# DoRA forward on one core: weights loaded first, weight preparation on 128 partitions, more buffers, equal blocks

## The chip, the core and the metric

The kernel runs on one core of a Trainium2 chip. The core has a matrix engine (TensorE, "PE" in the profile, its weight loads as "PEld"), a vector engine (VectorE, "DVE"), a scalar engine (ScalarE, "ACT"), GpSimd ("POOL") and a synchronising engine ("SP"). Matrix results go to PSUM, everything else lives in SBUF; transfers between SBUF and the chip's main memory are done by 16 DMA engines. In this kernel two engines issue transfers: SP, whose transfers the profile shows as queue q1, and ACT, whose transfers are q10. The metric is the device time of one execution in microseconds (us); smaller is better.

## The reference

```python
# x: 16 x 2048 x 256, W: 256 x 256, lora_A: 256 x 16, lora_B: 16 x 256, m: 256, scale = 1.0, all float32
W_adapted = W + scale * (lora_A @ lora_B)
W_norm = np.sqrt(np.sum(W_adapted ** 2, axis=0, keepdims=True) + 1e-8)
W_final = W_adapted / W_norm * m
y = x.reshape(-1, 256) @ W_final          # 32768 x 256 times 256 x 256
```

The input x and the output y have 33.55 MB each. The weights have 0.28 MB together. So the kernel reads x once, writes y once, and multiplies by a small matrix that it must first prepare.

## The kernel before

**Weight preparation.** Four transfers bring `lora_A` (`a_nat`, as 256 pieces of 64 bytes), `W` (`w_nat`, 256 pieces of 1 KB), `lora_B` (`b_nat`) and `m` (`m_row`, one row on one partition). PE transposes `a_nat` (L92), multiplies with `lora_B` (L98), DVE adds `W` (L107, `wa`), ACT squares (L112), PE sums over the rows with a column of ones (L115, one row of 256 sums on one partition), ACT takes the square root (L119), DVE the reciprocal (L120) and the product with `m` (L121), PE spreads the row over 128 partitions with a row of ones (L123), and DVE multiplies `wa` by it (L127) into `w_final`, 128 x 2 x 256 in bf16.

**Main loop.** x is cut into blocks. A full block is 2048 rows (2 MB): each of 128 partitions takes 16 consecutive rows, so one contiguous piece of 16 KB. A block is loaded by one transfer on SP (L71 for the first, L141 for the others) into one of the `xpool` buffers. It is worked off in groups of 4 rows per partition ("chunks", four to a full block, 64 in all). For each chunk PE makes 8 transposes (L151) into a PSUM tile `xt_ps` (two of them), DVE casts it to bf16 into `xt_sb` (L157, `xtpool` buffers), PE makes 8 matmuls with `w_final` (L162) into `y_ps` (two), and ACT copies it to the block's output tile `y_sb` (L169). After a block's last chunk ACT issues the store of the block (L171) out of one of the `ypool` buffers. Before, there are 4 load buffers, 12 `xt_sb` and 3 store buffers. The list `blocks` cuts the last 2048 rows into three pieces of 8, 4 and 4 rows per partition (pieces of 8 KB and 4 KB, `x_sb_1443`, `x_sb_1489` and `x_sb_1514` in the order below); the 15 blocks ahead of them are full. Blocks are counted from 0 here, chunks from 1.

**What sets the order.** The program is written block by block, and a scheduler turns it into one fixed list of instructions per engine. Each engine works its list strictly in order. The scheduler lets PE's transposes run ahead of the matmuls as far as the buffers reach: 12 `xt_sb` plus 2 `xt_ps` before. A transpose that waits for a load therefore also holds up the matmuls of older chunks that stand behind it. In the same way a copy on ACT that waits for a free `y_sb` buffer holds up everything behind it on ACT, and a load on SP waits until the transposes of the block that had its buffer are done.

Of the kernel before, what the change touches and what calls it, by code (L numbers as in the profile page):

```python
# [10 lines left out]
@with_exitstack  # L11
def kernel(
    ctx: ExitStack,
    tc: tile.TileContext,
    x: bass.AP,
    W: bass.AP,
    lora_A: bass.AP,
    lora_B: bass.AP,
    m: bass.AP,
    scale: float,  # L20
    out: bass.AP,
):
# [22 lines left out]
    off = (NBLK - n_tail) * DJ  # L45
    tail_js = n_tail * DJ
    pieces = [8] * (tail_js // 8 - 1) + [4, 4]
    for dj in pieces:
        blocks.append((off * P, dj))
        off += dj  # L50
# [9 lines left out]
    identity = consts.tile([P, P], FP32)  # L60
    make_identity(nc, identity)
    ones_col = consts.tile([P, 1], FP32)
    nc.vector.memset(ones_col, 1.0)  # L63
    ones_row = consts.tile([1, P], FP32)
    nc.vector.memset(ones_row, 1.0)

    w_final = consts.tile([P, KC, OUT], BF16)

    x_sb_first = xpool.tile([P, DJ, IN], FP32, name="x_sb", tag="x_sb")
    dj0 = blocks[0][1]  # L70
    nc.sync.dma_start(  # L71
        out=x_sb_first[:, :dj0, :],
        in_=x_flat[0 : dj0 * P].rearrange("(p j) k -> p j k", p=P),
    )
# [9 lines left out]
    eps_1 = startup.tile([1, 1], FP32)  # L84
    nc.vector.memset(eps_1, 1e-8)

    b_bf = startup.tile([R, OUT], BF16)
    nc.vector.tensor_copy(out=b_bf, in_=b_nat)

    aT_ps = pp_y.tile([R, KC * P], FP32, tag="psy", name="aT_ps")  # L90
    for c in range(KC):
        nc.tensor.transpose(aT_ps[:, c * P : (c + 1) * P], a_nat[:, c, :], identity)  # L92
    aT = startup.tile([R, KC * P], BF16)
    nc.vector.tensor_copy(out=aT, in_=aT_ps)  # L94

    ab_ps = pp_y.tile([P, KC, OUT], FP32, tag="psy", name="ab_ps")
    for c in range(KC):
        nc.tensor.matmul(  # L98
            ab_ps[:, c, :],
            aT[:, c * P : (c + 1) * P],  # L100
            b_bf,
            start=True,
            stop=True,
        )

    wa = startup.tile([P, KC, OUT], FP32)
    nc.vector.scalar_tensor_tensor(  # L107
        out=wa, in0=ab_ps, scalar=float(scale), in1=w_nat, op0=ALU.mult, op1=ALU.add
    )
# [4 lines left out]
    for c in range(KC):  # L114
        nc.tensor.matmul(  # L115
            n2_ps, ones_col, sq[:, c, :], start=(c == 0), stop=(c == KC - 1)
        )
    d_row = startup.tile([1, OUT], FP32)
    nc.scalar.activation(out=d_row, in_=n2_ps, func=AF.Sqrt, bias=eps_1)  # L119
    nc.vector.reciprocal(out=d_row, in_=d_row)  # L120
    nc.vector.tensor_mul(out=d_row, in0=d_row, in1=m_row)  # L121
    db_ps = pp_y.tile([P, OUT], FP32, tag="psy", name="db_ps")
    nc.tensor.matmul(db_ps, ones_row, d_row, start=True, stop=True)  # L123
    d_bcast = startup.tile([P, OUT], FP32)
    nc.vector.tensor_copy(out=d_bcast, in_=db_ps)  # L125
    for c in range(KC):
        nc.vector.tensor_mul(out=w_final[:, c], in0=wa[:, c], in1=d_bcast)  # L127

    j_order = []
    for a in range(J // 2):  # L130
        j_order.append(a)
        j_order.append(a + J // 2)

    for s0, dj in blocks:
        nsub = dj // J

        if s0 == 0:
            x_sb = x_sb_first
        else:
            x_sb = xpool.tile([P, DJ, IN], FP32, name="x_sb", tag="x_sb")  # L140
            nc.sync.dma_start(  # L141
                out=x_sb[:, :dj, :],
                in_=x_flat[s0 : s0 + dj * P].rearrange("(p j) k -> p j k", p=P),
            )
        y_sb = ypool.tile([P, DJ, OUT], FP32, name="y_sb")

        for c in range(nsub):
            xt_ps = pp_xt.tile([P, KC, J * P], FP32, tag="psxt", name="xt_ps")
            for j in range(J):
                for kc in range(KC):  # L150
                    nc.tensor.transpose(  # L151
                        xt_ps[:, kc, j * P : (j + 1) * P],
                        x_sb[:, c * J + j, kc * P : (kc + 1) * P],
                        identity,
                    )
            xt_sb = xtpool.tile([P, KC, J * P], BF16, name="xt_sb")
            nc.vector.tensor_copy(out=xt_sb, in_=xt_ps)  # L157

            y_ps = pp_y.tile([P, J, OUT], FP32, tag="psy", name="y_ps")
            for kc in range(KC):  # L160
                for j in j_order:
                    nc.tensor.matmul(  # L162
                        y_ps[:, j, :],
                        xt_sb[:, kc, j * P : (j + 1) * P],
                        w_final[:, kc, :],
                        start=(kc == 0 and (j % (J // 2)) == 0),
                        stop=(kc == KC - 1 and (j % (J // 2)) == (J // 2) - 1),
                    )
            nc.scalar.copy(out=y_sb[:, c * J : (c + 1) * J, :], in_=y_ps)  # L169

        nc.scalar.dma_start(  # L171
            out=out_flat[s0 : s0 + dj * P].rearrange("(p j) k -> p j k", p=P),
            in_=y_sb[:, :dj, :],
        )


# [33 lines left out]
```

## Time and profile before

| What | us |
|---|---|
| Median of 3 runs (lowest, highest) | 174.78 (174.4, 175.59) |
| Span of the profiled execution, first to last instruction | 172.6 |
| Median less that span | 2.2 |
| PE busy / DVE busy / ACT busy | 131.4 / 80.1 / 65.5 |
| First matmul with the finished weights | 24.93 |
| First store issued | 30.11 |
| PE's last wait for a load ends | 142.90 |
| Last store issued | about 168.0 |

The profiled execution has no time of its own on record beside its span; what lies around the span is taken as the difference to the median, 2.2 us (1.8 to 3.0 by the lowest and highest run). In the profile's strip of 40 slices a slice is 4.3 us wide and a digit is the busy share in tenths. In rows of a timeline the first number is the start, the second the time to the end of the group, and what stands in brackets is the idle time of the engine ahead of it and what ended it.

### The profile page before, as it was taken

How to read it: one execution, taken by the hardware profiler on the slowest of the kernel's cores; microseconds unless marked ns; L12 is line 12 of the kernel's file. 1: busy time of each engine (PE TensorE's matmuls, PEld its weight loads, DVE VectorE, ACT ScalarE, POOL GpSimd, SP SyncE). 2: the span in 40 equal slices, each digit the busy share in tenths (PEclk: the TensorE clock that was granted, in tenths of full speed). 3: DMA queues.
4: the chain of work that ended last, by engine and by line, in shares of the span. 5: the costliest groups of instructions: out<-in, count | busy, mean ns of one | idle time of the engine just before them, and what ended most of it. 6: DMA issues, size and time to landing. Idle time of an engine off the chain costs nothing.

```text
span 172.6 us, 2407 instructions
## 1 busy us (share of the span) xinstructions
PE 131.4 (76%) x1034; PEld 109.6 (64%) x1034; DVE 80.1 (46%) x75; ACT 65.5 (38%) x68; POOL 0.7 (0%) x6
## 2 busy tenths in 40 slices
PE   0089589899998989989898989889689408898300
PEld 0077468777786878868787878777578407676200
DVE  0046991792948558465555656565355500500000
ACT  2004008417062350807180808163428000898320
POOL 1000000000000000000000000000000000000000
PEclk9999999999999999999999999999999855999955
DMA  5999999999999999999999999999999970299985
GB/s 179 415 417 425 429 433 421 421 429 433 421 418 418 429 425 425 429 435 425 429 429 425 425 444 429 423 425 429 431 426 418 446 299 0 122 421 421 433 345 206
DMA packets 5772, 67.55 MB, mean 391 GB/s; under 512 B 881, under 2 KB 1154, under 8 KB 1666
## 3 DMA queue, kind: packets, MB, share of 16 engines
q1 hardware_dynamic: 2898, 33.84, 46.8%
q10 hardware_dynamic: 2864, 33.57, 45.9%
q8 instruction: 8, 0.13, 0.3%
q14 instruction: 2, 0.02, 0.0%
HBM read 33.85 MB, written 33.55 MB: 391 GB/s over the span
## 4 chain that ended last, share of the span: by engine, by line
PE 50%; DMA 24%; DVE 14%; ACT 7%; issue 2%; ACTq 0%
PE xt_ps L151 25%; PE y_ps L162 24%; DMA x_sb<-in_x_dram 14%; DVE xt_sb L157 13%; ACT y_sb L169 7%; DMA out_dram<-y_sb 5%; DMA a_nat<-in_lora_A_dram 5%; DVE d_row L120 1%; PE n_ps L115 1%; PE db_ps L123 0%; PE aT_ps L92 0%; PE ab_ps L98 0%; ACTq L171 0%; ACTq L169 0%
## 5 line engine op out<-in xcount | busy, mean ns | idle before, releaser
L157 DVE CAST xt_sb<-xt_ps 128x1024 bf16<-128x1024 f32 x64 | 76.0, 1220 | 59.5 <-PE xt_ps L151 33.1
L169 ACT COPY y_sb<-y_ps 128x1024 f32<-128x1024 f32 x64 | 61.9, 1015 | 88.5 <-PE y_ps L162 78.1
L151 PE MATMUL xt_ps<-identity,x_sb 128*128 128x128 f32 x512 | 72.3, 286 | 17.4 <-DVE xt_sb L157 8.5
L151 PEld LDWEIGHTS xt_ps<-identity,x_sb 128*128 128x128 f32 x512 | 59.1, 146 | 28.0 <-DVE xt_sb L157 19.9
L162 PE MATMUL y_ps<-w_final,xt_sb 128*128 128x256 bf16 x512 | 63.7, 276 | 3.3 <-ACT y_sb L169 3.3
L162 PEld LDWEIGHTS <-xt_sb 128*128 128x128 bf16 x512 | 50.6, 99 | 13.3 <-issue 6.4
L92 PE MATMUL aT_ps<-identity,a_nat 128*16 128x128 f32 x2 | 0.6, 394 | 9.1 <-DMA a_nat<-in_lora_A_dram 9.1
L92 PEld LDWEIGHTS aT_ps<-identity,a_nat 128*16 128x16 f32 x2 | 0.1, 90 | 9.1 <-issue 9.1
L112 ACT ACTIVATE sq<-wa 128x512 f32<-128x512 f32 x1 | 0.6, 631 | 10.8 <-DVE wa L107 10.8
L94 DVE CAST aT<-aT_ps 16x256 bf16<-16x256 f32 x1 | 0.4, 412 | 8.7 <-PE aT_ps L92 8.7
L112 ACT ACT_TABLE_LOAD x1 | 1.3, 1283 | 1.2 <-PEq L191 1.2
L120 DVE RECIPROCAL d_row<-d_row 1x256 f32<-1x256 f32 x1 | 1.7, 1730 | 0.0
L119 ACT ACT_TABLE_LOAD x1 | 1.3, 1283 | 0.0
L119 ACT ACTIVATE d_row<-n_ps,eps 1x256 f32<-1x256 f32 x1 | 0.5, 465 | 1.9 <-PE n_ps L115 1.9
L115 PE MATMUL n_ps<-sq,ones_col 128*1 128x256 f32 x4 | 1.0, 378 | 0.0
L127 DVE TENSOR_TENSOR w_final<-wa,d_bcast 128x256 bf16<-128x256 f32 x2 | 0.8, 417 | 0.0
L123 PE MATMUL db_ps<-d_row,ones_row 1*128 1x256 f32 x2 | 0.7, 426 | 0.0
L107 DVE SCALAR_TENSOR_TENSOR wa<-ab_ps,w_nat 128x512 f32<-128x512 f32 x1 | 0.7, 681 | 0.0
L98 PE MATMUL ab_ps<-b_bf,aT 16*128 16x256 bf16 x2 | 0.6, 402 | 0.0
L115 PEld LDWEIGHTS n_ps<-sq,ones_col 128*1 128x1 f32 x4 | 0.3, 82 | 0.4 <-issue 0.2
L63 DVE MEMSET ones_col<- 128x1 f32 x1 | 0.1, 59 | 0.8 <-PEq L191 0.8
L125 DVE COPY d_bcast<-db_ps 128x256 f32<-128x256 f32 x1 | 0.4, 402 | 0.0
(12 smaller groups left out, 2.2 us busy)
## 6 DMA issues: line engine op xcount, KB each, us to landing
x_sb<-in_x_dram SPq DMA_DIRECT2D x15, 2048.0 KB, 16.2
out_dram<-y_sb ACTq DMA_DIRECT2D x15, 2048.0 KB, 15.1
x_sb<-in_x_dram SPq DMA_DIRECT2D x1, 1024.0 KB, 28.2
x_sb<-in_x_dram SPq DMA_DIRECT2D x2, 512.0 KB, 24.9
out_dram<-y_sb ACTq DMA_DIRECT2D x1, 1024.0 KB, 9.2
out_dram<-y_sb ACTq DMA_DIRECT2D x2, 512.0 KB, 3.7
w_nat<-in_W_dram SPq DMA_DIRECT2D x1, 256.0 KB, 8.2
a_nat<-in_lora_A_dram ACTq DMA_DIRECT2D x1, 16.0 KB, 8.3
```

What stands on the lines that cost most here:

```text
L92: nc.tensor.transpose(aT_ps[:, c * P : (c + 1) * P], a_nat[:, c, :], identity)
L107: nc.vector.scalar_tensor_tensor(out=wa, in0=ab_ps, scalar=float(scale), in1=w_nat, op0=ALU.mult, op1=ALU.add)
L112: nc.scalar.activation(out=sq, in_=wa, func=AF.Square)
L115: nc.tensor.matmul(n2_ps, ones_col, sq[:, c, :], start=(c == 0), stop=(c == KC - 1))
L119: nc.scalar.activation(out=d_row, in_=n2_ps, func=AF.Sqrt, bias=eps_1)
L120: nc.vector.reciprocal(out=d_row, in_=d_row)
L123: nc.tensor.matmul(db_ps, ones_row, d_row, start=True, stop=True)
L127: nc.vector.tensor_mul(out=w_final[:, c], in0=wa[:, c], in1=d_bcast)
L151: nc.tensor.transpose(xt_ps[:, kc, j * P : (j + 1) * P], x_sb[:, c * J + j, kc * P : (kc + 1) * P], identity,)
L157: nc.vector.tensor_copy(out=xt_sb, in_=xt_ps)
L162: nc.tensor.matmul(y_ps[:, j, :], xt_sb[:, kc, j * P : (j + 1) * P], w_final[:, kc, :], start=(kc == 0 and (j % (J // 2)) == 0), stop=(kc ...
L169: nc.scalar.copy(out=y_sb[:, c * J : (c + 1) * J, :], in_=y_ps)
```

## The change

Transfers: `w_nat` is issued first on SP, ahead of the first block of x. `b_nat` and `m_row` move from SP to ACT's queue, behind `a_nat`.

Weight preparation: it is scheduled with high priority. `m` is spread over 128 partitions at once by a product of one row of ones with `m_row` (L92, `mb_ps`, copied to `m_all` at L94). The square is done by DVE (L111). The sum over rows is done with a full 128 x 128 matrix of ones (L116), so that every partition holds all 256 sums; the square root (L120) and the reciprocal (L125) then run on 128 partitions, and the second spreading product is gone. `wa` times `m` (L123, `wam`) is computed ahead of the reciprocal, and `w_final` is `wam` times the reciprocal (L127). ACT makes one square root on a dummy (L77) at the start, which loads its function table there.

Buffers: six load buffers for four, five store buffers for three, six `xt_sb` for twelve. Blocks: all 16 are full blocks; the three small pieces at the end are gone. Nothing else of the main loop is changed (transposes L142, casts L148, matmuls L153, copies L160, stores L162, loads L53 in the new numbering).

```diff
-    n_tail = min(1, NBLK)
-    blocks = [(i * BLK, DJ) for i in range(NBLK - n_tail)]
...
-    pieces = [8] * (tail_js // 8 - 1) + [4, 4]
...
-    xpool = ctx.enter_context(tc.tile_pool(name="xpool", bufs=4))
-    xtpool = ctx.enter_context(tc.tile_pool(name="xtpool", bufs=12))
-    ypool = ctx.enter_context(tc.tile_pool(name="ypool", bufs=3))
+    xpool = ctx.enter_context(tc.tile_pool(name="xpool", bufs=6))
+    xtpool = ctx.enter_context(tc.tile_pool(name="xtpool", bufs=6))
+    ypool = ctx.enter_context(tc.tile_pool(name="ypool", bufs=5))
...
-    nc.sync.dma_start(out=b_nat, in_=lora_B)
+    nc.scalar.dma_start(out=b_nat, in_=lora_B)
     m_row = startup.tile([1, OUT], FP32)
-    nc.sync.dma_start(out=m_row, in_=m[None, :])
...
+    nc.scalar.dma_start(out=m_row, in_=m[None, :])
...
+    ones = consts.tile([P, P], FP32)
+    nc.vector.memset(ones, 1.0)
...
+    nc.scalar.activation(out=warm, in_=eps_col, func=AF.Sqrt)
...
+    with tc.high_priority():
...
+        mb_ps = pp_y.tile([P, OUT], FP32, tag="psy", name="mb_ps")
+        nc.tensor.matmul(mb_ps, ones[0:1, :], m_row, start=True, stop=True)
+        m_all = startup.tile([P, OUT], FP32)
+        nc.vector.tensor_copy(out=m_all, in_=mb_ps)
...
-    sq = startup.tile([P, KC, OUT], FP32)
-    nc.scalar.activation(out=sq, in_=wa, func=AF.Square)
-    n2_ps = pp_y.tile([1, OUT], FP32, tag="psy", name="n2_ps")
...
+        sq = startup.tile([P, KC, OUT], FP32)
+        nc.vector.tensor_mul(out=sq, in0=wa, in1=wa)
...
+        n2_ps = pp_y.tile([P, OUT], FP32, tag="psy", name="n2_ps")
+        for c in range(KC):
+            nc.tensor.matmul(
+                n2_ps, ones, sq[:, c, :], start=(c == 0), stop=(c == KC - 1)
+            )
+        norm = startup.tile([P, OUT], FP32)
+        nc.scalar.activation(out=norm, in_=n2_ps, func=AF.Sqrt, bias=eps_col)
+        wam = startup.tile([P, KC, OUT], FP32)
+        for c in range(KC):
+            nc.vector.tensor_mul(out=wam[:, c], in0=wa[:, c], in1=m_all)
+        rnorm = startup.tile([P, OUT], FP32)
+        nc.vector.reciprocal(out=rnorm, in_=norm)
+        for c in range(KC):
+            nc.vector.tensor_mul(out=w_final[:, c], in0=wam[:, c], in1=rnorm)
...
-    for s0, dj in blocks:
...
+    for b in range(NBLK):
+        x_sb = load_x(b)
```

Three places of the fixed lists are used below: SP's list, the start of PE's list and the end of PE's list. First SP's list from its start, which holds only transfers (`128x4096` is a full block, `128x2048` and `128x1024` are the small pieces):

```order
-L71 DMA x_sb<-in_x_dram 128x4096
-L79 DMA w_nat<-in_W_dram 128x2x256
-L81 DMA b_nat<-in_lora_B_dram 16x256
-L83 DMA m_row<-in_m_dram 1x256
-L141 DMA x_sb<-in_x_dram 128x4096 x14
-L141 DMA x_sb<-in_x_dram 128x2048
-L141 DMA x_sb<-in_x_dram 128x1024 x2
-L205 UNCONDITIONAL_BRANCH
+L196 UNCONDITIONAL_BRANCH
+L63 DMA w_nat<-in_W_dram 128x2x256
+L53 DMA x_sb<-in_x_dram 128x4096 x16
```

The first block now stands behind `w_nat`, the two small transfers have left SP, and the last 2048 rows come as one load.

Second, PE's list from its start up to the first matmul with the finished weights, before (`x8` and the like count rows that follow each other):

```order
L92 MATMUL aT_ps<-identity,a_nat 16x128 x2
L151 MATMUL xt_ps<-identity,x_sb 128x128 x8
L98 LDWEIGHTS aT
L98 MATMUL ab_ps<-b_bf,aT 128x256
L98 LDWEIGHTS aT
L98 MATMUL ab_ps<-b_bf,aT 128x256
L151 MATMUL xt_ps<-identity,x_sb 128x128 x23
L115 MATMUL n_ps<-sq,ones_col 1x256 x2
L151 MATMUL xt_ps<-identity,x_sb 128x128 x20
L123 MATMUL db_ps<-d_row,ones_row 128x256
L151 MATMUL xt_ps<-identity,x_sb 128x128 x15
```

and now:

```order
L87 MATMUL aT_ps<-identity,a_nat 16x128 x2
L92 MATMUL mb_ps<-m_row,ones 128x256
L98 LDWEIGHTS aT
L98 MATMUL ab_ps<-b_bf,aT 128x256
L98 LDWEIGHTS aT
L98 MATMUL ab_ps<-b_bf,aT 128x256
L142 MATMUL xt_ps<-identity,x_sb 128x128 x9
L116 MATMUL n_ps<-sq,ones 128x256 x2
L142 MATMUL xt_ps<-identity,x_sb 128x128 x18
```

Before, 66 transposes of x stand ahead of the first matmul with the weights, spread between the steps of the preparation; now 27 do, and all of them stand behind the product that needs `m_row` (L92).

Third, the place on PE where the transposes of the last rows stand, before. `y_ps_1214` is the 50th of 64 chunks, and the last row of it is the first row here; `x_sb_1514` is the last piece loaded; `y_ps_1235` is chunk 51.

```order
L162 MATMUL y_ps_1214<-w_final_85,xt_sb_1212 128x256
L151 MATMUL xt_ps_1446<-identity_76,x_sb_1443 128x128 x7
L151 MATMUL xt_ps_1467<-identity_76,x_sb_1443 128x128 x8
L151 MATMUL xt_ps_1492<-identity_76,x_sb_1489 128x128 x8
L151 MATMUL xt_ps_1517<-identity_76,x_sb_1514 128x128 x8
L162 LDWEIGHTS xt_sb_1233
L162 MATMUL y_ps_1235<-w_final_85,xt_sb_1233 128x256
```

All transposes of the last piece stand ahead of chunk 51, so 14 chunks' matmuls wait for the last load.

And the same place now. `y_ps_1305` is the 54th chunk, `x_sb_1358` is block 14, `x_sb_1446` is block 15, the last one, and `y_ps_1326` is chunk 55.

```order
L153 MATMUL y_ps_1305<-w_final_95,xt_sb_1303 128x256
L142 MATMUL xt_ps_1403<-identity_84,x_sb_1358 128x128 x7
L142 MATMUL xt_ps_1424<-identity_84,x_sb_1358 128x128 x8
L142 MATMUL xt_ps_1449<-identity_84,x_sb_1446 128x128 x8
L142 MATMUL xt_ps_1470<-identity_84,x_sb_1446 128x128 x8
L153 LDWEIGHTS xt_sb_1324
L153 MATMUL y_ps_1326<-w_final_95,xt_sb_1324 128x256
```

The first transposes of the last block now stand behind chunk 54, so 10 chunks' matmuls stand behind the last load, and 13 blocks' stores (52 chunks) ahead of it.

More of the change, by code (lines that the diff above doesn't have):

```diff
@@ L41, with load_x @@
     assert IN % P == 0 and OUT % P == 0 and N % BLK == 0
[L43 to L50 removed]
     consts = ctx.enter_context(tc.tile_pool(name="consts", bufs=1))
     startup = ctx.enter_context(tc.tile_pool(name="startup", bufs=1))
[L54 to L56 removed]
+    xpool = ctx.enter_context(tc.tile_pool(name="xpool", bufs=6))
+    xtpool = ctx.enter_context(tc.tile_pool(name="xtpool", bufs=6))
+    ypool = ctx.enter_context(tc.tile_pool(name="ypool", bufs=5))
     pp_xt = ctx.enter_context(tc.tile_pool(name="pp_xt", bufs=2, space=bass.MemoryType.PSUM))
     pp_y = ctx.enter_context(tc.tile_pool(name="pp_y", bufs=2, space=bass.MemoryType.PSUM))
[L60 to L74, printed above, removed]
+    def load_x(b):
+        t = xpool.tile([P, DJ, IN], FP32, name="x_sb", tag="x_sb")
+        nc.sync.dma_start(
+            out=t,
+            in_=x_flat[b * BLK : (b + 1) * BLK].rearrange("(p j) k -> p j k", p=P),
+        )
+        return t
     a_nat = startup.tile([P, KC, R], FP32)
@@ L93 @@
[L93 to L103, printed above, removed]
-        )
[L106 to L109, printed above, removed]
@@ L111 @@
-    sq = startup.tile([P, KC, OUT], FP32)
-    nc.scalar.activation(out=sq, in_=wa, func=AF.Square)
-    n2_ps = pp_y.tile([1, OUT], FP32, tag="psy", name="n2_ps")
[L114 to L127, printed above, removed]
+    nc.scalar.dma_start(out=m_row, in_=m[None, :])
+    identity = consts.tile([P, P], FP32)
+    make_identity(nc, identity)
+    ones = consts.tile([P, P], FP32)
+    nc.vector.memset(ones, 1.0)
@@ new lines @@
+    eps_col = startup.tile([P, 1], FP32)
+    nc.vector.memset(eps_col, 1e-8)
+    warm = startup.tile([P, 1], FP32)
+    nc.scalar.activation(out=warm, in_=eps_col, func=AF.Sqrt)
+    w_final = consts.tile([P, KC, OUT], BF16)
+    with tc.high_priority():
+        b_bf = startup.tile([R, OUT], BF16)
+        nc.vector.tensor_copy(out=b_bf, in_=b_nat)
+        aT_ps = pp_y.tile([R, KC * P], FP32, tag="psy", name="aT_ps")
+        for c in range(KC):
+            nc.tensor.transpose(aT_ps[:, c * P : (c + 1) * P], a_nat[:, c, :], identity)
+        aT = startup.tile([R, KC * P], BF16)
+        nc.vector.tensor_copy(out=aT, in_=aT_ps)
+        mb_ps = pp_y.tile([P, OUT], FP32, tag="psy", name="mb_ps")
+        nc.tensor.matmul(mb_ps, ones[0:1, :], m_row, start=True, stop=True)
+        m_all = startup.tile([P, OUT], FP32)
+        nc.vector.tensor_copy(out=m_all, in_=mb_ps)
+        ab_ps = pp_y.tile([P, KC, OUT], FP32, tag="psy", name="ab_ps")
+        for c in range(KC):
+            nc.tensor.matmul(
+                ab_ps[:, c, :],
+                aT[:, c * P : (c + 1) * P],
+                b_bf,
+                start=True,
+                stop=True,
+            )
+        wa = startup.tile([P, KC, OUT], FP32)
+        nc.vector.scalar_tensor_tensor(
+            out=wa, in0=ab_ps, scalar=float(scale), in1=w_nat, op0=ALU.mult, op1=ALU.add
+        )
+        sq = startup.tile([P, KC, OUT], FP32)
+        nc.vector.tensor_mul(out=sq, in0=wa, in1=wa)
+        n2_ps = pp_y.tile([P, OUT], FP32, tag="psy", name="n2_ps")
+        for c in range(KC):
+            nc.tensor.matmul(
+                n2_ps, ones, sq[:, c, :], start=(c == 0), stop=(c == KC - 1)
+            )
+        norm = startup.tile([P, OUT], FP32)
+        nc.scalar.activation(out=norm, in_=n2_ps, func=AF.Sqrt, bias=eps_col)
+        wam = startup.tile([P, KC, OUT], FP32)
+        for c in range(KC):
+            nc.vector.tensor_mul(out=wam[:, c], in0=wa[:, c], in1=m_all)
+        rnorm = startup.tile([P, OUT], FP32)
+        nc.vector.reciprocal(out=rnorm, in_=norm)
+        for c in range(KC):
+            nc.vector.tensor_mul(out=w_final[:, c], in0=wam[:, c], in1=rnorm)
@@ L132 @@
         j_order.append(a + J // 2)
-    for s0, dj in blocks:
[L135 to L144, printed above, removed]
+    for b in range(NBLK):
+        x_sb = load_x(b)
         y_sb = ypool.tile([P, DJ, OUT], FP32, name="y_sb")
-        for c in range(nsub):
+        for c in range(DJ // J):
             xt_ps = pp_xt.tile([P, KC, J * P], FP32, tag="psxt", name="xt_ps")
@@ L171 @@
         nc.scalar.dma_start(
-            out=out_flat[s0 : s0 + dj * P].rearrange("(p j) k -> p j k", p=P),
-            in_=y_sb[:, :dj, :],
+            out=out_flat[b * BLK : (b + 1) * BLK].rearrange("(p j) k -> p j k", p=P),
+            in_=y_sb,
         )
```

7 lines of the change are left out of this document (removed).

## The prediction

> **What bounds the kernel now.** I read the page's strips first, for the engine that is never idle.
>
> ```profile
> span 172.6 us, 2407 instructions
> DMA  5999999999999999999999999999999970299985
> GB/s 179 415 417 425 429 433 421 421 429 433 421 418 418 429 425 425 429 435 425 429 429 425 425 444 429 423 425 429 431 426 418 446 299 0 122 421 421 433 345 206
> DMA packets 5772, 67.55 MB, mean 391 GB/s; under 512 B 881, under 2 KB 1154, under 8 KB 1666
> ```
>
> The DMA engines are full from the second slice on, at some 425 GB/s, with one hole near the end (the digits 7, 0, 2: about 138 to 150 us). 67.55 MB must move whatever the order. So time is lost where DMA is not full: the start, the hole, the end. To size the hole I counted bytes per queue in stretches (packets, MB, share of 16 engines; q1 loads, q10 stores; in this order 0 to 30 us, 62 to 115 in three rows, 118 to 141.5 in two, 141.5 to 149.5, 150 to 155).
>
> ```profile
> DMA packets 1351, 11.65 MB, mean 388 GB/s; under 512 B 385, under 2 KB 658, under 8 KB 658
> ...
> DMA packets 1568, 22.69 MB, mean 428 GB/s; under 512 B 182, under 2 KB 182, under 8 KB 182
> q1 hardware_dynamic: 793, 11.58, 51.2%
> q10 hardware_dynamic: 770, 11.04, 48.9%
> ...
> q10 hardware_dynamic: 506, 7.37, 73.5%
> q1 hardware_dynamic: 468, 2.47, 25.2%
> ...
> DMA packets 15, 0.07 MB, mean 9 GB/s; under 512 B 10, under 2 KB 10, under 8 KB 11
> ...
> DMA packets 142, 2.08 MB, mean 416 GB/s; under 512 B 15, under 2 KB 15, under 8 KB 15
> ```
>
> From 62 to 115 us loads and stores take turns packet by packet (793 to 770) and, with equal packets of 16 KB, share the bytes evenly. From 118 to 141.5 they still take turns (468 to 506), but the loads are now the small pieces, whose packets are 4 and 8 KB: they get a quarter of the bytes. So the last 2.47 MB of x take 23.5 us, while the stores run dry. Between 141.5 and 149.5 nothing moves: 8 us. Why, the timeline of that place tells.
>
> ```profile
> 136.80 1.60 PE L151 MATMUL xt_ps<-identity,x_sb 128*128 128x128 f32 x8 [2.29 <-DMA x_sb<-in_x_dram]
> 142.90 1.94 PE L151 MATMUL xt_ps<-identity,x_sb 128*128 128x128 f32 x8 [4.49 <-DMA x_sb<-in_x_dram]
> 144.63 4.14 PE L162 MATMUL y_ps<-w_final,xt_sb 128*128 128x256 bf16 x24
> 148.98 0.34 ACTq L171 DMA_DIRECT2D out_dram<-y_sb  x1
> ...
> 166.99 1.36 ACTq L171 DMA_DIRECT2D out_dram<-y_sb  x2
> ```
>
> PE stands at the last piece's transposes until 142.90, with 14 chunks of finished inputs behind them in its list (7.3 MB of output not yet computed). The next store is issued at 148.98, and all 7.3 MB are then written with no load beside them. The chain is: small packets, late last load, PE's list held up, DMA empty.
>
> **The change part by part.** *Floor.* The start moves the same bytes, so I keep 11.65 MB by 30 us. 67.55 − 11.65 = 55.9 MB remain. While loads and stores mix, 0.428 MB/us; after the last load, stores alone at 0.416 (2.08 MB in 5 us). If stores begin to flow at 26.5 (below), loads have then 11.65 − 3.5 × 0.428 − 0.29 (weights) = 9.9 MB, and the other 23.7 MB take turns with stores at 11.58/53 = 0.2185 MB/us: 108 us, so the last load's data end near 135. From 30 to 135 that is 44.9 MB, and the last 11.0 MB take 26.4 us: 161.4. The row before the strip's end gives 1.3 us from the last packet to the end of the span:
>
> ```profile
> DMA packets 3, 0.01 MB, mean 16 GB/s; under 512 B 1, under 2 KB 1, under 8 KB 3
> ```
>
> (that is 171 to 171.5, and nothing after it, in a span of 172.6). So a span of 162.7 if DMA is never empty. At 0.416 throughout it would be 2.9 us more.
>
> *Weights first.* Who comes when at the start, by issue and size, and in packets (windows 3 to 4, 4 to 5, 7.75 to 8 and 0 to 23 us):
>
> ```profile
> x_sb<-in_x_dram SPq DMA_DIRECT2D x1, 2048.0 KB, 7.8
> a_nat<-in_lora_A_dram ACTq DMA_DIRECT2D x1, 16.0 KB, 8.3
> ...
> q10 hardware_dynamic: 5, 0.00, 0.3%
> ...
> q1 hardware_dynamic: 28, 0.46, 108.3%
> q10 hardware_dynamic: 29, 0.00, 2.0%
> ...
> q1 hardware_dynamic: 69, 0.06, 72.0%
> q10 hardware_dynamic: 63, 0.00, 17.1%
> ...
> q10 hardware_dynamic: 272, 0.02, 0.8%
> ```
>
> Both are issued at 0.74. `a_nat` needs 272 packets (256 pieces and 16 completions) and gets one turn for each 16 KB packet of x, about 27 a microsecond; only once `w_nat`'s 1 KB pieces alternate with it does it go fast (132 packets in 0.25 us). It landed at 9.0. With `w_nat` ahead, those two alternate from the first: I take 1.3 us for the first packets and 1.2 for the rest, then some three left-over turns, 0.6 us each (16 engines, 28 packets a microsecond); all three are estimates, and rival A is their other end: `a_nat` at about 6, `b_nat` 7, `m_row` 8.2. The first block lands at 0.74 + 7.8 + 1.2 (`w_nat`'s share) = 9.8. PE's first transposes of x stand behind the `m_row` product and L98 and start at 9.9. The two issues moved to ACT delay only its table load; ACT has nothing before the square root. Fifth and sixth load are issued earlier, and DMA has a queue anyway: nothing.
>
> ```profile
> 9.52 1.91 PE L151 MATMUL xt_ps<-identity,x_sb 128*128 128x128 f32 x8
> 24.93 1.92 PE L162 MATMUL y_ps<-w_final,xt_sb 128*128 128x256 bf16 x16
> 30.11 0.36 ACTq L171 DMA_DIRECT2D out_dram<-y_sb  x1
> ...
> L120 DVE RECIPROCAL d_row<-d_row 1x256 f32<-1x256 f32 x1 | 1.7, 1730 | 0.0
> L119 ACT ACTIVATE d_row<-n_ps,eps 1x256 f32<-1x256 f32 x1 | 0.5, 465 | 1.9 <-PE n_ps L115 1.9
> L115 PE MATMUL n_ps<-sq,ones_col 128*1 128x256 f32 x4 | 1.0, 378 | 0.0
> L127 DVE TENSOR_TENSOR w_final<-wa,d_bcast 128x256 bf16<-128x256 f32 x2 | 0.8, 417 | 0.0
> L157 DVE CAST xt_sb<-xt_ps 128x1024 bf16<-128x1024 f32 x64 | 76.0, 1220 | 59.5 <-PE xt_ps L151 33.1
> ```
>
> *Preparation.* 128 partitions by 256 cost what the rows of 256 cost on one partition, since the row length is the same (two-sided bound: half or double of 1.7 us for the reciprocal, −0.9 or +1.7). From 9.9: nine transposes at the slow first rate 2.2, the sums 1.0, square root 0.5, reciprocal 1.7, one cast ahead of L127 in DVE's list 1.2, two products 0.8: first matmul at 17.3 (24.93 before). Adding `W`, the square and `wam` run beside the transposes. From the first matmul to the first store it was 5.2; 11 more transposes stand between now, 1.5 (their price is worked out below): store at 24.0, 6 us earlier. By itself this ends nothing sooner, since DMA is full of loads meanwhile.
>
> *Buffers and order.* How fast PE and ACT can supply stores, from three issues of stores (numbers 1, 5 and 9):
>
> ```profile
> 40.20 0.34 ACTq L171 DMA_DIRECT2D out_dram<-y_sb  x1
> 80.31 0.34 ACTq L171 DMA_DIRECT2D out_dram<-y_sb  x1
> 113.49 0.34 ACTq L171 DMA_DIRECT2D out_dram<-y_sb  x1
> ACT y_sb L169 <- DMA out_dram<-y_sb: 9.9, 4, 3.8
> ```
>
> 10.03 us a block early (the casts, 1.22 a chunk, bound the long runs of transposes), 8.30 later. Two chunks' matmuls took 1.92 at 24.93, so a chunk's are 0.96, and the 32 transposes of a block take 8.30 − 4 × 0.96 = 4.46 with their waits. The new list has the same two patterns, the second from block 4 on. So, unheld, the last store is issued at 24.0 + 4 × 10.03 + 11 × 8.30 − 2.2 (16 transposes missing at the end) = 153.2. The issue at 148.98, alone on DMA, and the two at the end took this long to land:
>
> ```profile
> out_dram<-y_sb ACTq DMA_DIRECT2D x1, 2048.0 KB, 6.9
> ...
> out_dram<-y_sb ACTq DMA_DIRECT2D x2, 512.0 KB, 3.7
> ```
>
> The last was issued at about 168.0, so it landed at 171.7, 0.9 ahead of the end of the span. A lone last store thus needs 7.8, and 162.7 holds if it is issued by 154.9: 1.7 us to spare. The last block's transposes come up two chunks and 16 transposes, 4.1 us, after store 12 (24.0 + 40.1 + 8 × 8.30 + 4.1 = 134.6); its data land at about 136: a wait of 1.4 us. At 135 thirteen stores have been issued and (135 − 26.5) × 11.04/53 = 22.6 MB, 10.8 of them, written: 2.2 blocks or 10.8 us of work bridge the gap to store 13 at 139. The 9.9 us that ACT waited for three store buffers go: with five, block 15 needs store 10, done at 136, at 149. Six `xt_sb` for twelve cost nothing while the pattern is kept, and shorten what waits behind the last load from 14 to 10 chunks.
>
> *Equal blocks.* The last load keeps 16 KB packets, so its half of the turns is half of the bytes. The last store is 2 MB in place of 0.5; alone at the end it costs 6.9 against 3.7 us, but it stands in a queue that is full until then, so nothing.
>
> Sum: span 162.7 against 172.6, so 9.9 us less; with the 2.2 us between span and median, 164.9: forecast **165**. The profiled span stands 2.2 below the median and 1.8 below the fastest run.
>
> [...] The measured row is 29 turns of q10 to 28 of q1 in a microsecond. [...]
>
> **The rivals.** *A: the weights starve behind x.* q10's first packets came only after 3 us although it was issued with q1. If that lateness is its own and not due to packets of x already taken in, `w_nat` is through when it starts, and every piece of `a_nat` waits for 16 KB of x: 3.3 + 272/27 + 0.7 = 14.1, `b_nat` 15.3, `m_row` 16.5, and transposes of x at 17.8, 7.9 late. The last store goes out at 161.1, and 7.8 more: span 168.9, time **171**. For it the five packets in 3 to 4 us; against it that whole 16 KB packets stood ahead.
>
> *B: the last load is late again.* If stores win more than their half, all 13 are written before it lands: (33.8 + 27.3 − 11.65)/0.428 after 30 is 145.6, landing 146.6. PE then works from cold as at 142.90 (16 transposes 3.9, three chunks 4.1); seven more chunks are 6.7, the last transposes 2.2, a copy 1.0: last store at 164.5, span 172.3, time **174.5**, no change. Against it: 793 to 770.
>
> *C, slower: starvation at two turns to one.* If q10 gets one turn for two of x, its 272 packets take 20 us: `a_nat` 24, `b_nat` 26.5, `m_row` 29, transposes at 30.2, 20.3 late, last store at 173.5, span 181.3, time **183.5**. It makes the kernel slower by 1% once `m_row` lands after 21.8. Against it the even turns of 4 to 5 us.
>
> *D: a hole from another cause* (a store kept back on ACT, PE slower than 8.30 beside more transfers): 167 to 175.
>
> **How the numbers follow.** Main case 0.62, A 0.19, B 0.08, C 0.05, D 0.06. The main case alone spans 163.5 (1.5 us less: a tail without the 1.3 us) to 167.9 (0.416 MB/us). The range 163.5 to 172 takes in A; left out are B, C and a part of D. 1% is 1.7 us, about what three runs (1.2 us apart) can tell. Faster by over 1%: the main case, A and most of D, 0.85. Within 1%: B and the rest of D, 0.1. Slower: C, 0.05.
>
> **What would show it.** Right: a DMA strip without a hole ahead of its last slice, the first matmul with the weights near 17, the first store near 24, the last wait for a load over by 137, no wait of ACT for store buffers, stores alone in the last 25 us. `a_nat` landing past 12 is A or C, a zero in the strip after the last load B. Wrong altogether would be loads and stores that mix below 0.41 MB/us, or a PE block time above 9 us in the second half.

## The result and the profile after

The changed kernel takes 165.96 us (median; 165.79 to 166.14), the kernel before, on the same chip, 175.19 us (174.4 to 176.06). The ratio is 0.947, with a 95% interval of 0.941 to 0.953. The forecast was 165.0, with a range of 163.5 to 172. The profiled execution took 166.08 us with a span of 164.3, so 1.8 us lie around the span. Medians here and below are of all runs of a kernel; where some of them lie more than 1.5% above its fastest, the ratio and its interval leave these out.

The page of the changed kernel, its strips and the issue of `a_nat` (KB, us from issue to landing; a slice is 4.1 us):

```profile
span 164.3 us, 2402 instructions
DMA  5999999999999999999999999999999999999991
GB/s 156 430 435 435 427 431 335 423 435 431 423 431 431 435 419 435 429 423 427 443 431 419 427 435 439 413 431 439 431 423 431 435 431 423 431 427 435 423 419 76
...
a_nat<-in_lora_A_dram ACTq DMA_DIRECT2D x1, 16.0 KB, 3.0
```

The hole is gone: every slice between the first and the last has a 9. `a_nat` lands 3.0 us after its issue, where it took 8.3. Two smaller losses are new to the eye: one slice with 335 GB/s (24.6 to 28.7 us) and a last slice with 76.

The timeline of the same kernel, with the places that the prediction priced: the `m_row` product, the first transposes of x, the first matmul with the weights, the first store, the last wait for a load, the last transposes, and the last four stores.

```profile
7.37 1.19 PE L92 MATMUL mb_ps<-m_row,ones 1*128 1x256 f32 x2 [2.88 <-DMA m_row<-in_m_dram]
9.22 2.18 PE L142 MATMUL xt_ps<-identity,x_sb 128*128 128x128 f32 x9 [0.23 <-DMA x_sb<-in_x_dram]
...
16.93 1.91 PE L153 MATMUL y_ps<-w_final,xt_sb 128*128 128x256 bf16 x16
23.87 0.38 ACTq L162 DMA_DIRECT2D out_dram<-y_sb  x1
...
134.02 0.34 ACTq L162 DMA_DIRECT2D out_dram<-y_sb  x1
...
138.99 1.94 PE L142 MATMUL xt_ps<-identity,x_sb 128*128 128x128 f32 x16 [2.21 <-DMA x_sb<-in_x_dram]
...
143.80 0.34 ACTq L162 DMA_DIRECT2D out_dram<-y_sb  x1
...
144.76 1.80 PE L142 MATMUL xt_ps<-identity,x_sb 128*128 128x128 f32 x15
...
149.61 0.34 ACTq L162 DMA_DIRECT2D out_dram<-y_sb  x1
153.69 0.34 ACTq L162 DMA_DIRECT2D out_dram<-y_sb  x1
```

The last wait for a load is 2.2 us instead of 4.5. While it lasts, DMA still has stores to write, because the store at 134.02 is already the thirteenth. The windows by queue say the same (62 to 115 us in three rows, then two rows of 135 to 140):

```profile
DMA packets 1551, 22.77 MB, mean 430 GB/s; under 512 B 160, under 2 KB 160, under 8 KB 160
q10 hardware_dynamic: 778, 11.44, 50.6%
q1 hardware_dynamic: 768, 11.27, 49.8%
...
q10 hardware_dynamic: 132, 1.90, 88.8%
q1 hardware_dynamic: 32, 0.26, 12.4%
```

Loads and stores share evenly as before. All but 0.03 MB of the loads are through at 137 us, and the stores go on alone at the full rate (6.44 MB from 145 to 160 us).

### The profile page after: what moved, and what is told of

It reads as the page before. It is cut to its first block, busy times and chain, and to the rows that moved or that the text cites. A ratio compares the mean times of both kernels' runs of the same rounds, so it can differ in the third digit from the quotient of the medians.

```text
span 164.3 us, 2402 instructions
## 1 busy us (share of the span) xinstructions
PE 128.1 (78%) x1034; PEld 110.6 (67%) x1034; DVE 81.1 (49%) x76; ACT 63.8 (39%) x67; POOL 0.7 (0%) x6
## 4 chain that ended last, share of the span: by engine, by line
PE 41%; DMA 34%; DVE 10%; ACT 6%; issue 1%; SPq 0%
DMA x_sb<-in_x_dram 34%; PE y_ps L153 20%; PE xt_ps L142 20%; DVE xt_sb L148 9%; ACT y_sb L160 6%; DVE rnorm L125 1%; PE n_ps L116 1%; ACT norm L120 0%; SPq L63 0%
## 5 line engine op out<-in xcount | busy, mean ns | idle before, releaser
L148 DVE CAST xt_sb<-xt_ps 128x1024 bf16<-128x1024 f32 x64 | 75.6, 1219 | 57.9 <-PE y_ps L153 29.1
L160 ACT COPY y_sb<-y_ps 128x1024 f32<-128x1024 f32 x64 | 61.9, 1015 | 78.2 <-PE y_ps L153 70.0
L142 PE MATMUL xt_ps<-identity,x_sb 128*128 128x128 f32 x512 | 70.4, 284 | 14.0 <-DMA x_sb<-in_x_dram 8.0
L142 PEld LDWEIGHTS xt_ps<-identity,x_sb 128*128 128x128 f32 x512 | 59.6, 146 | 21.3 <-DVE xt_sb L148 18.3
L153 PE MATMUL y_ps<-w_final,xt_sb 128*128 128x256 bf16 x512 | 62.8, 273 | 3.8 <-ACT y_sb L160 2.9
L153 PEld LDWEIGHTS <-xt_sb 128*128 128x128 bf16 x512 | 49.8, 98 | 12.7 <-issue 5.7
L120 ACT ACTIVATE norm<-n_ps,eps_col 128x256 f32<-128x256 f32 x1 | 0.5, 473 | 9.3 <-PE n_ps L116 9.3
L92 PE MATMUL mb_ps<-m_row,ones 1*128 1x256 f32 x2 | 1.2, 693 | 2.9 <-DMA m_row<-in_m_dram 2.9
L92 PEld LDWEIGHTS mb_ps<-m_row,ones 1*128 1x128 f32 x2 | 0.5, 309 | 3.3 <-DVE aT L89 3.3
L125 DVE RECIPROCAL rnorm<-norm 128x256 f32<-128x256 f32 x1 | 1.8, 1754 | 1.2 <-ACT norm L120 1.2
L116 PE MATMUL n_ps<-sq,ones 128*128 128x256 f32 x4 | 1.9, 635 | 0.0
L94 DVE COPY m_all<-mb_ps 128x256 f32<-128x256 f32 x1 | 0.4, 424 | 2.2 <-PE mb_ps L92 2.2
L116 PEld LDWEIGHTS n_ps<-sq,ones 128*128 128x128 f32 x4 | 1.2, 336 | 0.2
L123 DVE TENSOR_TENSOR wam<-wa,m_all 128x256 f32<-128x256 f32 x2 | 0.8, 418 | 0.0
L127 DVE TENSOR_TENSOR w_final<-wam,rnorm 128x256 bf16<-128x256 f32 x2 | 0.7, 414 | 0.0
L111 DVE TENSOR_TENSOR sq<-wa 128x512 f32<-128x512 f32 x1 | 0.7, 692 | 0.0
```

Of the source, the lines that this page charges most:

```text
L92: nc.tensor.matmul(mb_ps, ones[0:1, :], m_row, start=True, stop=True)
L111: nc.vector.tensor_mul(out=sq, in0=wa, in1=wa)
L116: nc.tensor.matmul(n2_ps, ones, sq[:, c, :], start=(c == 0), stop=(c == KC - 1))
L123: nc.vector.tensor_mul(out=wam[:, c], in0=wa[:, c], in1=m_all)
L125: nc.vector.reciprocal(out=rnorm, in_=norm)
L142: nc.tensor.transpose(xt_ps[:, kc, j * P : (j + 1) * P], x_sb[:, c * J + j, kc * P : (kc + 1) * P], identity,)
```

## The experiments

Stores are counted from 0 here as blocks are, so the first is store 0. Each ratio is to the kernel before, run on the same chip, which stood at about 175 us.

### One part alone: equal blocks, the weights, the buffers

**Equal blocks alone.** The kernel before, with the last 2048 rows as one block.

```diff
-    n_tail = min(1, NBLK)
-    blocks = [(i * BLK, DJ) for i in range(NBLK - n_tail)]
...
+    blocks = [(i * BLK, DJ) for i in range(NBLK)]
```

> The kernel before with one part of the change alone: 16 equal blocks, no small pieces (old weights, old buffers). Theory 'hole' (the time is 67.5 MB of transfers plus the time in which DMA is empty, and the hole came from small load packets that got a quarter of the bytes): the last load lands near 131 in place of 142.8, while two blocks of stores are still queued, so the strip has no empty slice and the time is 166 to 168. Rival 'early stores' (the weights, six us earlier, are what pays): 174 to 176, as before. Rival 'buffers' (the 9.9 us of waits for store buffers are what pays): 174 to 176.

Measured 168.77 us (167.53 to 170.68), ratio 0.962 (0.955 to 0.970). That is just above the range of theory 'hole' and far below both rivals, which foresaw no gain. The strip has no empty slice, as the theory says, yet the kernel is 2.8 us above the whole change.

**The weights alone.** The kernel before, with the new order of transfers and the new preparation, but with its own blocks and buffers.

```diff
-    nc.sync.dma_start(out=b_nat, in_=lora_B)
+    nc.scalar.dma_start(out=b_nat, in_=lora_B)
...
+    with tc.high_priority():
...
+        n2_ps = pp_y.tile([P, OUT], FP32, tag="psy", name="n2_ps")
```

> The kernel before with the weights' part alone (w_nat first, b_nat and m_row on ACT, preparation on 128 partitions, old blocks and buffers). Theory 'hole': first store near 24, but the last load still lands at 141 to 144 and DMA is empty for some 8 us after it: 174 to 176. Rival 'early stores': 6 us less, 168 to 170. Rival 'buffers': 174 to 176.

Measured 168.58 us (168.37 to 169.08), ratio 0.964 (0.958 to 0.970). I had written that this part ends nothing sooner by itself. That is wrong, and so is theory 'hole', which gave 174 to 176; rival 'early stores' gave 168 to 170.

**The buffers alone.** The kernel before, with three numbers changed.

```diff
-    xpool = ctx.enter_context(tc.tile_pool(name="xpool", bufs=4))
-    xtpool = ctx.enter_context(tc.tile_pool(name="xtpool", bufs=12))
-    ypool = ctx.enter_context(tc.tile_pool(name="ypool", bufs=3))
+    xpool = ctx.enter_context(tc.tile_pool(name="xpool", bufs=6))
+    xtpool = ctx.enter_context(tc.tile_pool(name="xtpool", bufs=6))
+    ypool = ctx.enter_context(tc.tile_pool(name="ypool", bufs=5))
```

> The kernel before with the buffers alone (6 load, 6 xt_sb, 5 store; old weights, small pieces at the end). Theory 'hole': the last pieces still get a quarter of the bytes and land at 140 to 144, but 10 chunks in place of 14 stand behind them and more stores are queued, so the hole shrinks to 2 to 6 us: 168 to 172. Rival 'buffers': all of the gain, 165 to 167. Rival 'early stores': 174 to 176.

Measured 165.92 us (165.81 to 166.21), ratio 0.949 (0.942 to 0.955): three numbers give the whole gain. Its strip, on the page, with the small pieces still in the program:

```profile
span 164.1 us, 2408 instructions
DMA  5999999999999999999999999999999999999992
```

So small packets alone do not make the hole. The three parts alone save 6.2, 6.4 and 9.0 us, together 21.6, where the whole change saves 9.2: all three work on the same loss.

### One part left out

**Without equal blocks** (weights and buffers).

```diff
+    pieces = [8] * (tail_js // 8 - 1) + [4, 4]
+    for dj in pieces:
+        blocks.append((off * P, dj))
...
-    for b in range(NBLK):
+    for s0, dj in blocks:
```

> The changed kernel with the small pieces at the end put back (new weights, new buffers). Theory 'hole': a hole of 2 to 6 us returns after the last load, 168 to 172, the same as the buffers alone within 1%. Rivals 'buffers' and 'early stores': 165 to 167, as the changed kernel, since the last store is smaller and nothing else is lost.

Measured 168.67 us, but from 166.49 to 170.47; ratio 0.954 (0.945 to 0.963). The scatter is as large as the question, so this run settles only that most of the gain is there without equal blocks. Its profiled execution (166.49 us) shows that the small pieces can still come late beside early stores. PE waits for the last one until 148.38, and the next store is issued at 152.49:

```profile
148.38 1.06 PE L148 MATMUL xt_ps<-identity,x_sb 128*128 128x128 f32 x8 [3.15 <-DMA x_sb<-in_x_dram]
...
152.49 0.34 ACTq L168 DMA_DIRECT2D out_dram<-y_sb  x1
```

From 148 to 152.5 us DMA moves 1.31 MB, 291 GB/s on the mean: a small hole, about 1.4 us of work. That the buffers alone, with the same small pieces, do not scatter (165.81 to 166.21) was not followed up.

**Without the weights** (equal blocks and buffers; the preparation as before).

```diff
-    nc.scalar.dma_start(out=b_nat, in_=lora_B)
+    nc.sync.dma_start(out=b_nat, in_=lora_B)
...
-    with tc.high_priority():
```

> The changed kernel with the old weights' part put back (equal blocks and new buffers stay). Theory 'queue' (the end is reached when all bytes have moved, so only a moment in which no store and no load is queued costs time; anything that is late earlier is made up): first store near 32.5, the strip stays full, 165 to 167. Rival, the prediction's sum of the supply (store 15 unheld at 153.2 with 1.7 us to spare): 8 us later at the start make 5 to 6 us at the end, 170 to 172.

Measured 165.86 us (165.82 to 166.0), ratio 0.948 (0.943 to 0.953), against 165.96 for the whole change, as theory 'queue' has it. The earlier weights bring nothing once the hole is closed otherwise.

**Without the buffers** (equal blocks and weights).

```diff
-    xpool = ctx.enter_context(tc.tile_pool(name="xpool", bufs=6))
-    xtpool = ctx.enter_context(tc.tile_pool(name="xtpool", bufs=6))
-    ypool = ctx.enter_context(tc.tile_pool(name="ypool", bufs=5))
+    xpool = ctx.enter_context(tc.tile_pool(name="xpool", bufs=4))
+    xtpool = ctx.enter_context(tc.tile_pool(name="xtpool", bufs=12))
+    ypool = ctx.enter_context(tc.tile_pool(name="ypool", bufs=3))
```

> The changed kernel with the old buffers put back (4 load, 12 xt_sb, 3 store; new weights and equal blocks stay). Theory 'queue': the last load keeps half of the bytes and lands at 134 to 139, so 14 chunks behind it wait little, 166 to 168. Rival 'order of PE' (what counts is how many chunks stand behind the last load, 14 against 6 to 10): a hole of some us, 169 to 172.

Measured 169.98 us (169.65 to 170.74), ratio 0.972 (0.967 to 0.978). That is the range of rival 'order of PE'. Here the forecast's main cause (small packets) is removed and the weights are early, and still 4 us are missing. On its page the hole is back, shorter (the digits 5, 5, 9, 9, 9, 9, 1 end the strip):

```profile
DMA  6999999999999999999999999999999995599991
GB/s 178 437 436 428 416 412 342 432 432 428 424 436 432 428 432 432 434 432 409 436 424 432 432 428 430 428 436 428 436 428 432 424 420 233 230 393 428 436 436 74
```

### Which of the three numbers

**Six `xt_sb` alone**, in the kernel before.

```diff
-    xtpool = ctx.enter_context(tc.tile_pool(name="xtpool", bufs=12))
+    xtpool = ctx.enter_context(tc.tile_pool(name="xtpool", bufs=6))
```

> The kernel before with 6 xt_sb in place of 12 and nothing else. Theory 'order of PE' (with fewer xt_sb the list lets PE run ahead less: 6 chunks in place of 14 stand behind the last piece, and the faster pattern of 8.3 us a block begins with the second block): the hole closes to under 2 us, 166 to 168. Rival 'load and store buffers' (six loads ahead or five stores are what closed it): 174 to 176.

Measured 167.3 us (166.48 to 169.23), ratio 0.955 (0.948 to 0.961). That is the range of theory 'order of PE'. Its profiled execution was the longest of the four (169.23 us), so little is taken from it: the strip, and the waits of ACT for one of the three store buffers (us, count, longest):

```profile
DMA  6999996799999999999999999999999999999983
ACT y_sb L169 <- DMA out_dram<-y_sb: 34.8, 9, 5.7
```

There is no hole ahead of the end. What this execution loses, it loses between 25 and 38 us: from 28 to 30 us DMA moves 0.02 MB, and the first store comes at 32.33. The buffers alone have no such dip, so the six load buffers may be what prevents it; no run separates this, and whether the shorter executions have the dip is not known. ACT waits 34.8 us, against 9.9 before, and even this execution is shorter than all of the kernel before (173.58 to 175.71).

**Twelve `xt_sb` put back into the changed kernel** (and one store buffer less).

```diff
-    xtpool = ctx.enter_context(tc.tile_pool(name="xtpool", bufs=6))
-    ypool = ctx.enter_context(tc.tile_pool(name="ypool", bufs=5))
+    xtpool = ctx.enter_context(tc.tile_pool(name="xtpool", bufs=12))
+    ypool = ctx.enter_context(tc.tile_pool(name="ypool", bufs=4))
```

> The changed kernel with 12 xt_sb put back (and four store buffers in place of five, since five no longer fit beside them; six loads stay). Theory 'order of PE': 14 chunks stand behind the last load again, stores run dry before chunk 52 is done, a hole of 3 to 5 us, 169 to 172. Rival 'load and store buffers': 165 to 167.

Measured 170.31 us (170.17 to 170.5), ratio 0.974 (0.968 to 0.981): the same as without the buffers, and the range of theory 'order of PE'. That there are four store buffers and not five is not the cause: neither this kernel nor the one without the buffers has any wait of ACT for a store buffer. The timeline of its end shows why, beside the changed kernel's above:

```profile
135.00 0.34 ACTq L162 DMA_DIRECT2D out_dram<-y_sb  x1
136.55 0.30 PE L142 MATMUL xt_ps<-identity,x_sb 128*128 128x128 f32 x1 [1.40 <-DMA x_sb<-in_x_dram]
...
137.56 1.80 PE L142 MATMUL xt_ps<-identity,x_sb 128*128 128x128 f32 x15
139.80 2.22 PE L142 MATMUL xt_ps<-identity,x_sb 128*128 128x128 f32 x16 [0.45 <-DVE xt_sb L148]
...
144.89 0.34 ACTq L162 DMA_DIRECT2D out_dram<-y_sb  x1
```

The store at 135.00 is store 11 and that at 144.89 store 12. In the changed kernel the stores at nearly the same times, 134.02 and 143.80, are 12 and 13. With twelve `xt_sb` the transposes run so far ahead of the matmuls that all 32 of the last block (1 + 15 + 16) stand ahead of the end of block 12; with six, the second half of them (the row at 144.76) comes after store 13 is issued. From 116 us until the last store is issued, at least one block less has been handed to DMA at every moment.

**Six load buffers alone, five store buffers alone**, in the kernel before.

```diff
-    xpool = ctx.enter_context(tc.tile_pool(name="xpool", bufs=4))
+    xpool = ctx.enter_context(tc.tile_pool(name="xpool", bufs=6))
```

> The kernel before with six load buffers in place of four and nothing else. Theory 'order of PE': the list of PE stays, the last piece still lands late with 14 chunks behind it, 173 to 176. Rival 'load buffers': 165 to 169.

```diff
-    ypool = ctx.enter_context(tc.tile_pool(name="ypool", bufs=3))
+    ypool = ctx.enter_context(tc.tile_pool(name="ypool", bufs=5))
```

> The kernel before with five store buffers in place of three and nothing else. Theory 'order of PE': ACT's 9.9 us of waits for store buffers go, the end does not move, 173 to 176. Rival 'store buffers': 165 to 169.

Six load buffers: 172.69 us, but from 168.96 to 173.66 and without a usable interval; in its profiled execution (172.38 us) the hole is there. Whether they help a little stays open. Five store buffers: 175.28 us, ratio 1.000 (0.996 to 1.005). Nothing, although the waits of ACT for a store buffer are gone from its profile.

### The bound

**The transfers alone.** Loads into eleven buffers, and each block stored as it came; the weights, the matmuls and all else are left out.

```diff
-        y_sb = ypool.tile([P, DJ, OUT], FP32, name="y_sb")
...
-            in_=y_sb,
+            in_=x_sb,
```

> Transfers alone: the 16 equal blocks of x are loaded and stored again from the same buffers, 11 of them, with no weights and no computation (so the output is x). It measures the floor of 67.1 MB in this order of queues. If the changed kernel is bound by its transfers from start to end: 162 to 165, within 3 us of it. If computation still costs at its end: below 161.

Measured 162.62 us (162.56 to 162.84), ratio 0.930 (0.925 to 0.934), with a span of 160.8. The changed kernel is 3.3 us above that, a little more than the 3 us that were to show it bound by its transfers from start to end.

### What sets the hole

One small balance fits all of these. Take what has been handed to DMA by 135 us and what of it is moved; what is left is moved at 0.428 MB/us, and if the next store is issued after that, DMA stands still for the difference. For the kernel before, by the windows of 0 to 135 us (loads, then stores):

```profile
q1 hardware_dynamic: 2779, 33.43, 59.1%
q10 hardware_dynamic: 1833, 22.92, 40.0%
```

Twelve stores are issued by then, 25.17 MB, so 2.25 MB of them are left, and of the loads 33.83 − 33.43 = 0.40: DMA is empty 2.65/0.428 = 6.2 us later, at 141.2. The next store comes at 148.98: a hole of 7.8 us. The same for the others:

| Kernel | Stores issued by 135 | Stores written, MB | Loads left, MB | Empty at | Next store | Hole by this | Span above the changed kernel's |
|---|---|---|---|---|---|---|---|
| Before | 12 | 22.92 | 0.40 | 141.2 | 148.98 | 7.8 | 8.3 |
| Five store buffers | 12 | 22.71 | 0.51 | 141.9 | 149.75 | 7.8 | 9.1 |
| Changed, twelve `xt_sb` | 12 | 22.60 | 0.01 | 141.0 | 144.89 | 3.9 | 4.3 |
| Changed without the buffers | 12 | 22.55 | 0.01 | 141.1 | 144.56 | 3.5 | 4.1 |
| Weights alone | 12 (the twelfth, at 135.38, counted in) | 23.05 | 0.59 | 141.3 | 143.67 | 2.4 | 3.0 |
| Equal blocks alone | 12 | 21.51 | 0 | 143.5 | 143.10 | 0 | 2.6 |
| Buffers alone | 13 | 22.87 | 0.29 | 145.9 | 142.42 | 0 | −0.2 |
| Changed without the weights | 13 | 22.68 | 0 | 145.7 | 139.17 | 0 | −0.3 |
| Changed | 13 | 22.81 | 0.27 | 146.0 | 143.80 | 0 | 0 |

The hole explains the spans to within 1.3 us in all rows but one. Equal blocks alone have no hole; there the loss is that DMA moved 1.0 MB less by 135 us, 2.4 us of work, most of it between 36 and 60 us (why is open):

```profile
DMA packets 635, 9.36 MB, mean 390 GB/s; under 512 B 64, under 2 KB 64, under 8 KB 64
```

The column that separates the good kernels is the second: thirteen stores against twelve. The three kernels with thirteen have all three new numbers, so the table by itself cannot say which of them counts. That it is `xt_sb` rests on the two runs above: six of them alone bring 4.5%, and twelve put back beside six load buffers lose it again, without any wait for a store buffer. (Six `xt_sb` alone, six load buffers alone and without equal blocks are left out for their scatter; in the last of these the last load also comes long after 135 us.) The kernels with twelve differ in when store 12 comes: at 143 to 145 with an early last load or with early weights, at 149 to 150 without.

## Why the prediction was right, and where it was not

**The floor and the startup were right.** First transposes 9.22 (9.9 forecast), `m_row` product 7.37 (8.2), first matmul with the weights 16.93 (17.3), first store 23.87 (24.0), last store issued 153.69 (153.2). ACT's table load (L77, 1.28 us) ran from 2.34, well ahead of the square root at 13.15. The two patterns of the block, 10.03 and 8.30 us, hold for the first seven stores, the second from one block sooner than forecast. By 135 us 13 stores are issued and 22.81 MB written, as forecast (13 and 22.6), and they bridge the gap to store 13, though that came at 143.80 and not at 139. Two of these agreements are partly luck. The sums over the rows took 1.9 us (L116) where 1.0 was forecast, which a start 0.7 us earlier nearly hides: the reciprocal and the square root kept their price on 128 partitions (1.75 for 1.73, 0.47 for 0.47), the sums did not. And the last store met its time although store 13 was 5 us late: the last two blocks took 9.9 us together, since few transposes stood between their matmuls, where 14 were forecast.

**The rivals.** A and C (weights that starve) fall with `a_nat`'s landing 3.0 us after its issue. That is sooner than the forecast's own estimate of about 6. In the window 2 to 3 us the two queues share the turns while `w_nat` and `a_nat` are both under way:

```profile
q1 hardware_dynamic: 217, 0.29, 99.4%
q10 hardware_dynamic: 150, 0.01, 10.2%
```

So `w_nat`'s pieces of 1 KB and `a_nat`'s of 64 bytes go through side by side, 217 to 150, as forecast. That the turns are of single pieces this row alone does not show. B (the last load late again) did not come: its wait ended at 138.99, three us later than the forecast's 136 and past the 137 that was set as a sign, but with DMA still full. D's first form came and cost nothing: ACT was held at a store, and what ended the wait was a load (us, count, longest):

```profile
ACT y_sb L160 <- DMA x_sb<-in_x_dram: 5.0, 1, 5.0
```

Stores 7 and 8 go out at 90.33 and 100.05, 9.7 to 11.1 us after the one ahead of them where 8.30 was due. The row is that of store 8; for store 7 the profile names PE's transposes as what ended a wait of 3.2 us. Why a store should wait for a load is not shown. DMA was full the while, so no time is lost. No wait of ACT for a store buffer is left.

**Where it failed, step by step.**

- "Six `xt_sb` for twelve cost nothing while the pattern is kept, and shorten what waits behind the last load from 14 to 10 chunks." This was a half-sentence, with no time put to it. It is the step that carries the result: alone it gives a ratio of 0.955, and taken out of the full change it costs 4.4 us.
- "The chain is: small packets, late last load, PE's list held up, DMA empty." As a description of the kernel before it stands, but the links are not worth the same. With the small packets kept and six `xt_sb` there is no hole (buffers alone), or a small one when the weights are early (without equal blocks); with the small packets gone and twelve `xt_sb` there is one of 3.5 us (without the buffers). So the third link is worth more than the first. Cutting the first alone leaves no hole only where 3.66 MB of stores (25.17 − 21.51) are still queued at 135 us, because DMA had moved 1.0 MB less until then.
- "By itself this ends nothing sooner" (the weights). By itself it took off 6.4 us. Earlier stores mean that the stores run out earlier, which lets the last small loads through sooner. By 135 us eleven stores (23.07 MB) had been issued there and 23.05 MB were written. Two windows of 135 to 137 us show what follows, in the kernel with the weights alone,

```profile
q1 hardware_dynamic: 136, 0.50, 60.7%
q10 hardware_dynamic: 27, 0.29, 36.0%
```

  and in the kernel before:

```profile
q10 hardware_dynamic: 51, 0.62, 73.0%
q1 hardware_dynamic: 60, 0.22, 27.0%
```

  PE has no wait for the last pieces there, and store 12 comes at 143.67 instead of 148.98. With equal blocks the same early stores do not help: 168.77 alone, 169.98 with the weights added, by ratio 0.962 (0.955 to 0.970) and 0.972 (0.967 to 0.978). Nor do they in the full change.
- "The 9.9 us that ACT waited for three store buffers go." They went, and were worth nothing (five store buffers alone: 175.28 us).
- The sum was 162.7 for the span, and it was 164.3. By 135 us 56.49 MB had moved, where 56.55 were forecast: the dip at 24 to 29 us (last section) was nearly made up by then, since loads and stores together ran at 0.430 MB/us rather than 0.428. The 11.06 MB left would have ended at 160.8 and not at 161.4, since stores alone ran at 0.429 rather than 0.416. But the last packets came at 162.1 (last section), and 2.2 us in place of 1.3 lie between them and the end of the span. The 2.2 us around the span were 1.8. In all the forecast was 1 us short, inside its range.

The size of the gain came out because the change does all three things, and the closed hole was priced by the floor, for which it does not matter which of them closes it. As to which part pays, the forecast had it wrong.

## What to carry to other kernels

DMA was the bound here (430 GB/s from 62 to 115 us), and its moments with nothing queued explained the spans to within 1.3 us in all rows of the table but one. For a kernel like this, balance what has been handed to DMA against what is moved at the point where the loads end, and see when the next store is issued. Deeper buffers between two stages of an in-order list were not free: here they let the first stage run three blocks ahead, so that finished input waited while the store queue ran dry, and fewer buffers were 4.5% faster. A long wait was no sign of lost time: with six `xt_sb` alone ACT waited 34.8 us for a store buffer in an execution of 169.23 us, against 9.9 us in the kernel before, none of whose executions beside it took less than 173.58.

## What the runs showed that was not expected

- **Loads slow down for some us after an early first store.** Between 27 and 28 us of the changed kernel the same 16 engines move 0.26 MB, nearly all of it loads:

```profile
DMA packets 16, 0.26 MB, mean 262 GB/s; under 512 B 0, under 2 KB 0, under 8 KB 0
```

  Between 20 and 26 us the rate was 410 to 459. If all 16 engines are at work, a 16 KB packet takes about 1.0 us there (16 packets in a microsecond) in place of 0.6 (28 packets). By 30 us 11.36 MB are moved, where 11.65 were forecast: 0.7 us of work. The dip stands at the same place in all five profiles with a first store near 24 us (335 to 369 GB/s in that slice), as in the kernel without the buffers, above. With the buffers alone and the first store at 32.58, no slice from the third to the last but one is below 400. Its cause is open.
- **The transfers thin out at the end.** From 157 us to the end, 1.64 MB are left, 3.8 us at the full rate, and the strip of that window thins out after its middle (160.6 us):

```profile
DMA  4944986694494499669409002002000000000000
```

  The last packets come at 162.1, 1.3 us after the 160.8 at which a full rate would have ended. With the transfers alone the same strip (157 to 160.8) has no such thin stretch before its end at 159.1 us:

```profile
DMA  9884989884998988498984000000000000000000
```

  The changed kernel's span is 3.5 us longer than that of its transfers alone. At 135 us it has 11.06 MB left where they have 10.37 (1.6 us of work); the thin end makes 1.3 and the time behind the last packets 0.5. What thins the end was not tried, and the profile does not show the 16 engines one by one.
